# Gate and up of the last 1024 tokens by seven block products, with down as a stage of its own

## The chip, the cores and the metric

The kernel runs on one core of one Trainium2 chip. The metric is the device time of one launch in microseconds (us). Before the change three runs took 2739.67, 2743.64 and 2744.93 us; the median is 2743.64 us.

## The reference

One decoder layer on 2048 tokens of width 1024, all in float32. A token mixer (latent attention, a gated MLP in chunks, a short convolution) is followed by an output projection, and then a channel mixer:

```
h = rms_norm(x, ffn_pre_g)                                    # 2048 x 1024
f = (silu(h @ w_gate) * (h @ w_up)) @ w_down                  # 1024 -> 2816 -> 1024
x = x + rms_norm(f, ffn_post_g)
```

The change touches only this channel mixer, and only for tokens 1024 to 2047.

## The kernel before

Float32 accuracy is kept by splitting each operand into a high part and a rest (`hi_lo`, L164: ScalarE (ACT) rounds the high part, then VectorE (DVE) or GpSimd (POOL) subtracts it), and by three TensorE (PE) matmuls for each product: high x high, high x low, low x high (`mm3`, L203 to L205). A matmul here has 128 x 128 weights and 512 moving columns.

The stages follow each other: input projections, attention woven with the other mixers, the output projection and the first channel mixer (tokens 0 to 1023, `f0`), and then, from 1895 us on, the part that the change replaces or touches:

- `out_proj` for token tiles 8 to 15 (128 tokens each). For each tile it ends in `mix_post` (the normalised rows `h2`, L1038), eight transposes (L1045), two copies to `hT` (L1046) and a store to a DRAM tile `h2T_d` (L1048).
- `ffn(tail, 1, ...)`, called `f1`, for the 1024 tokens of tiles 8 to 15. `load_h2T` (L1129) reads `h2T_d` back and splits it into `h2T[0]` (tiles 8 to 11) and `h2T[1]` (tiles 12 to 15). Then eleven groups of two 128-wide column blocks j: `half` computes gate and up for one block and 512 tokens, 2 x 24 matmuls into PSUM tiles `gu`, then silu, product and split into `gT`. `down` multiplies the two blocks with `w_down` into PSUM tiles `pd` and adds each to an SBUF sum `acc` on DVE (L1173). Weights are read (L1116, L1139) and split once.
- `last_down` (L1203) has the last half and the last four token tiles: as each 512-wide piece of the output is complete, it is summed, squared, normalised and stored (L1233 to L1247).

All PE work of one half is 48 matmuls, so gate and up of these 1024 tokens are 22 blocks x 2 halves x 48 = 2112 matmuls, and down is 22 x 8 tiles x 2 x 3 = 1056.

Outside the places where an order is pinned, a list scheduler of the framework orders the instructions of each engine from its own estimate of times; each engine and each queue then runs its instructions strictly in that order and waits on semaphores. DMAs issued by SyncE (SP) are one such queue. Pools of SBUF tiles are opened on two sides; a tile that takes the place of an earlier one waits until that one has been used for the last time.

Of the kernel before, what the change touches and what calls it, by code (L numbers as in the profile page):

```python
# [11 lines left out]
F32 = mybir.dt.float32  # L12
F32R = mybir.dt.float32r
BF16 = mybir.dt.bfloat16
I32 = mybir.dt.int32
AF = mybir.ActivationFunctionType
ALU = mybir.AluOpType
AX = mybir.AxisListType

P = 128  # L20
S = 2048
D = 1024
KD = D // P
# [41 lines left out]
WB = 2  # L65
PAUSE3 = 8.0
WB1 = 1
H = 8
QR = 384
KVR = 256  # L70
FF = 2816
NF = FF // P
# [12 lines left out]
def trunk(  # L85
# [6 lines left out]
    nc = tc.nc  # L92
# [3 lines left out]
    x, out = x[0], out[0]  # L96
    w_in, w_uq, w_ukv, w_out = w_in[0], w_uq[0], w_ukv[0], w_out[0]
    w_gate, w_up, w_down = w_gate[0], w_up[0], w_down[0]

    const = ctx.enter_context(tc.tile_pool(name="const", bufs=1))  # L100
    dram = ctx.enter_context(tc.tile_pool(name="scratch", bufs=1, space=DRAM))
# [5 lines left out]
    def bank(tags, name):  # L107
        i = turn.get(tags, 0)
        turn[tags] = i + 1
        tag = tags[i % len(tags)]  # L110
        return psp.tile([P, 512], F32, name=name, tag=tag, bufs=BANKS[tag])
# [37 lines left out]
    hT_d = [dram.tile([P, 2, KD, P], F32R, name=f"hT_d{t}") for t in range(NT)]  # L149
    q_d = [dram.tile([H, 64, 2 * GT], F32R, name=f"q_d{c}") for c in range(S // GT)]  # L150
    qr_d = [dram.tile([P, 2, 2 * GT], F32R, name=f"qr_d{c}") for c in range(S // GT)]
    k_d = [dram.tile([H, 2, 96, 2, GT], F32R, name=f"k_d{c}") for c in range(NCH)]
    v_d = [dram.tile([P, 8, H, P], F32R, name=f"v_d{c}") for c in range(NCH // 2)]
    ya_d = [dram.tile([P, 2, 512], F32, name=f"ya_d{t}") for t in range(NT // 2)]
    ybc_d = [dram.tile([P, 512], F32, name=f"ybc_d{t}") for t in range(NT)]
    x2_d = [dram.tile([P, D], F32, name=f"x2_d{t}") for t in range(NT)]
    h2T_d = [dram.tile([P, KD, P], F32, name=f"h2T_d{t}") for t in range(NT)]
    trig_x = [dram.tile([H, 16, 2 * GT], F32, name=f"trig_x{c}") for c in range(S // GT)]
    trig_d = dram.tile([P, 2 * GT], F32, name="trig_d")

    def rows(t):
        return slice(t * P, (t + 1) * P)

    def hi_lo(hi, lo, src, eng=None):  # L164
        nc.scalar.activation(hi, src, AF.Copy)  # L165
        return (eng or nc.vector).tensor_tensor(lo, src, hi.bitcast(F32), op=ALU.subtract)  # L166

    def put(dst, src):
        nc.sync.dma_start(dst.bitcast(F32), src.bitcast(F32))

    def inv_rms(pool, ssq, n, width=1, bufs=8, eps=EPS, out=None):
        r = pool.tile([P, 4], F32, name="invr", tag="invr", bufs=bufs) if out is None else out
        nc.gpsimd.tensor_scalar(r[:, :width], ssq, 1.0 / n, eps, op0=ALU.mult, op1=ALU.add)
        nc.gpsimd.tensor_tensor(r[:, :width], r[:, :width], mhalf[:, :width], op=ALU.pow)
        return r
# [446 lines left out]
    with ExitStack() as ph:  # L622
# [31 lines left out]
        rp = rp_ctx.enter_context(tc.tile_pool(name="rope", bufs=1, side="right", reuse_waits="tile"))  # L654
# [618 lines left out]
                finish(t0, acc, range(ntc))  # L1273


    at_ctx = ctx.enter_context(ExitStack())
    at_pools.append(at_ctx.enter_context(tc.tile_pool(name="c_s", bufs=2, reuse_waits="tile")))
    next(rest)
# [3 lines left out]
    wo = []  # L1282
# [11 lines left out]
    with wo_ctx, ExitStack() as ph:  # L1294
        wo.append(wout_tiles(ph, 1, "d_wb", "right"))
        dsp = ph.enter_context(tc.tile_pool(name="d_s0", bufs=2, side="right", reuse_waits="tile"))
        gains = out_gains(ph, "d_g0", "right")
        dhp = ph.enter_context(tc.tile_pool(name="d_h0", bufs=1, side="right", reuse_waits="tile"))
        op0 = out_proj(dsp, dhp, None, wo, gains, range(0, 8), "z", "nx")
        next(op0)  # L1300
        wout_load(wo[1], 1, "d_stgb", "left", WB1)
        weave(op0, att, RATE1, LO_OUT, -PAUSE1)

    with ExitStack() as ph:
        def pools():
            return (ph.enter_context(tc.tile_pool(name="e_s0", bufs=2, side="right", reuse_waits="tile")),
                    ph.enter_context(tc.tile_pool(name="e_p0", bufs=1, side="right", reuse_waits="tile")))
# [6 lines left out]
        late = ctx.enter_context(ExitStack())  # L1314
        owed, wo = 0.0, None
# [11 lines left out]
        for cost in f0:  # L1327
            owed += RATE2 * cost
            while owed >= 1.0 and wo is None:
                owed -= 1.0  # L1330
                if not step(att):
                    wo, gains, dmp, mix = second_half()
        if wo is None:
            for _ in att:
                pass
            wo, gains, dmp, mix = second_half()

    with ExitStack() as tail:
        def pools():
            return (tail.enter_context(tc.tile_pool(name="e_s1", bufs=2, reuse_waits="tile")),  # L1340
                    tail.enter_context(tc.tile_pool(name="e_p1", bufs=1, reuse_waits="tile")))

        f1 = ffn(tail, 1, "right", (8,), 8, pools, "zszsz", "nox", False, 3)
        spare = next(f1)
        with ExitStack() as ph:
            dsp = ph.enter_context(tc.tile_pool(name="d_s1", bufs=2, side="right", reuse_waits="tile"))
            dhp = ph.enter_context(tc.tile_pool(name="d_h1", bufs=1, side="right", reuse_waits="tile"))
            op1 = out_proj(dsp, dhp, (dmp, spare[:, 3], mix), wo, gains, range(8, 16), "zzzs", "nox")
            next(op1)
            next(op1)  # L1350
            next(f1)
            for _ in op1:
                pass
        late.close()
        for _ in f1:
            pass
# [31 lines left out]
```

## Time and profile before

| | us |
|---|---|
| median of 3 runs | 2743.64 |
| the profiled execution, whole | 2746.96 |
| its span, first to last instruction | 2745.2 |
| PE busy in the span | 2651.7 (97%) |
| DVE, ACT, POOL busy | 1563.3, 1015.5, 727.0 |

A row of the timeline gives start, duration, engine, line, operation and, in brackets, the idle time before it with what ended it. PE's durations overlap: a matmul of 512 columns is shown with 0.39 us, while the next one starts 0.227 us later, so a pitch is read from two starts and never from a duration. Queue rows (SPq) show the issue of a DMA, not its transfer. In the profile the tiles `h2T0` and `h2T1` are both called `h2T`, and `x2` is `x`.

### The profile page before, as it was taken

What the parts mean: (1) busy time and instruction counts of PE and PEld (TensorE: products, weight loads), DVE (VectorE), ACT (ScalarE), POOL (GpSimd) and SP (SyncE); (2) the same over time, 40 slices, a digit from 0 to 9 for tenths busy, and PEclk for the clock granted to TensorE, in tenths of its full rate; (3) what the DMA queues carried; (4) which work ended last, traced back from release to release, by engine and by line L of the source; (5) the groups of instructions that cost most, each with busy time, mean ns of one, the idle gap of its engine ahead of it and who ended that gap; (6) DMA issues with size and microseconds to landing.
All of it is one profiled execution on the core that took longest, in us unless ns stands there. A gap on an engine that the chain in (4) does not pass through costs nothing. (4 is left out here: it accounts for less than half of the span.)

```text
span 2745.2 us, 37350 instructions
## 1 busy us (share of the span) xinstructions
PE 2651.7 (97%) x14076; PEld 2277.6 (83%) x14076; DVE 1563.3 (57%) x2709; ACT 1015.5 (37%) x1857; POOL 727.0 (26%) x828
## 2 busy tenths in 40 slices
PE   8999989999898999999999999999999999999998
PEld 7999868888777888888878888877878888888886
DVE  6555575566767666657677676764543333333335
ACT  6444344444546334444444444442531111111112
POOL 1222325666443232332343223313200000000004
PEclk9999979999999999999999999999999999999999
DMA  8756755444435332333253322254551111111113
GB/s 297 225 183 179 226 185 154 146 144 134 144 130 187 101 110 89 93 93 104 87 163 99 114 79 77 75 162 143 176 169 46 46 47 46 46 47 46 47 39 123
DMA packets 268945, 329.42 MB, mean 120 GB/s; under 512 B 17646, under 2 KB 198300, under 8 KB 264092
## 3 DMA queue, kind: packets, MB, share of 16 engines
q1 hardware_dynamic: 261244, 293.46, 34.5%
q0 software_dynamic: 5184, 29.36, 3.3%
q10 hardware_dynamic: 2336, 4.20, 0.4%
q8 instruction: 111, 1.82, 0.3%
q14 instruction: 70, 0.57, 0.1%
HBM read 238.56 MB, written 86.25 MB: 118 GB/s over the span
## 5 line engine op out<-in xcount | busy, mean ns | idle before, releaser
L476 POOL TENSOR_TENSOR pl<-p,ph 128x512 fp32r<-128x512 f32 (+1 forms) x240 | 325.8, 1362 | 636.8 <-ACT ph L473 542.2
L1173 DVE TENSOR_TENSOR acc<-pd,acc 128x512 f32<-128x512 f32 x304 | 206.1, 688 | 228.4 <-PE pd L205 227.9
L203 PE MATMUL gu<-h2T,wgh 128*128 128x512 f32 x704 | 275.1, 391 | 2.1 <-ACT h2T L165 2.1
L203 PE MATMUL gu<-h2T,wuh 128*128 128x512 f32 x704 | 275.2, 391 | 0.0
L204 PE MATMUL gu<-h2T,wgh 128*128 128x512 f32 x704 | 274.9, 391 | 0.1
L205 PE MATMUL gu<-h2T,wul 128*128 128x512 f32 x704 | 274.7, 390 | 0.0
L204 PE MATMUL gu<-h2T,wuh 128*128 128x512 f32 x704 | 274.7, 390 | 0.0
L205 PE MATMUL gu<-h2T,wgl 128*128 128x512 f32 x704 | 274.5, 390 | 0.0
L203 PE MATMUL pd<-wd,gT 128*128 128x512 f32 x672 | 265.0, 395 | 4.8 <-DVE acc L1173 2.7
L204 PE MATMUL pd<-wd,gT 128*128 128x512 f32 x672 | 262.3, 391 | 0.0
L205 PE MATMUL pd<-wd,gT 128*128 128x512 f32 x672 | 257.6, 392 | 0.3 <-DVE gT L166 0.3
L471 ACT ACTIVATE p<-sT 128x512 f32<-128x512 f32 (+1 forms) x288 | 163.3, 572 | 210.8 <-PE sT L205 120.7
L473 ACT ACTIVATE ph<-p 128x512 fp32r<-128x512 f32 (+1 forms) x288 | 174.2, 609 | 68.6 <-PE o L507 63.7
L1189 POOL DMA_DIRECT2D x<-x_d x8 | 4.7, 587 | 684.4 <-PE gu L205 683.1
L203 PE MATMUL sT<-zone 97*128 97x256 f32 x576 | 166.0, 288 | 7.5 <-ACT p L471 7.5
L435 DVE TENSOR_REDUCE mx<-s 128x1 f32<-128x512 f32 x192 | 130.2, 684 | 63.9 <-PE s L432 63.5
L205 PE MATMUL sT<-zone 97*128 97x256 f32 x576 | 165.1, 287 | 0.0
L204 PE MATMUL sT<-zone 97*128 97x256 f32 x576 | 165.0, 286 | 0.0
L507 PE MATMUL o<-pl,zone 128*128 128x256 f32 x576 | 151.5, 289 | 5.6 <-POOL pl L476 3.1
L165 ACT ACTIVATE gT<-sg 128x512 fp32r<-128x512 f32 x88 | 55.2, 627 | 274.4 <-DVE sg L1159 253.1
L203 PEld LDWEIGHTS gu<-h2T,wgh 128*128 128x128 f32 x704 | 132.3, 188 | 29.1 <-ACT h2T L165 2.5
L205 PEld LDWEIGHTS gu<-h2T,wul 128*128 128x128 f32 x704 | 132.5, 188 | 27.8
(280 smaller groups left out, 6293.2 us busy)
## 6 DMA issues: line engine op xcount, KB each, us to landing
raw<-in_w_gate_dram SPq DMA_DIRECT2D x66, 512.0 KB
raw<-in_w_up_dram SPq DMA_DIRECT2D x66, 512.0 KB
raw_d<-in_w_down_dram SPq DMA_DIRECT2D x66, 512.0 KB
ht<-hT_d POOLq DMA_DIRECT2D x20, 1024.0 KB, 5.7
zone<-k_d SPq DMA_DIRECT2D x48, 384.0 KB
hT_d<-ht SPq DMA_DIRECT2D x16, 1024.0 KB
xt<-in_x_dram SPq DMA_DIRECT2D x31, 512.0 KB
zone<-v_d SPq DMA_DIRECT2D x24, 512.0 KB
```

Source lines behind the costliest of these rows:

```text
L165: nc.scalar.activation(hi, src, AF.Copy)
L203: nc.tensor.matmul(ps, ah(k), bh(k), start=k == 0, stop=False)
L204: nc.tensor.matmul(ps, ah(k), bl(k), start=False, stop=False)
L205: nc.tensor.matmul(ps, al(k), bh(k), start=False, stop=k == n - 1)
L435: nc.vector.tensor_reduce(mx[:, b:b + 1], s[:, :w], axis=AX.X, op=ALU.max, negate=True)
L471: nc.scalar.activation(p[:, :w], s[:, :w], AF.Exp)
L473: nc.scalar.activation(ph_[:, :w], p[:, :w], AF.Copy)
L476: eng.tensor_tensor(pl_[:, :w], p[:, :w], ph_[:, :w].bitcast(F32), op=ALU.subtract)
L507: nc.tensor.matmul(o[:, at:256], vts[part, hd, j // 8][:, j % 8, :], pp[i][:, u * 256:u * 256 + 256 - at], start=j == 0 and i == 0, stop=j ...
L1173: nc.vector.tensor_tensor(acc[tt][:, cols], pd, acc[tt][:, cols], op=ALU.add)
L1189: nc.gpsimd.dma_start(x2, x2_d[t0 + tt])
```

## The change

`f1` is now `wide_ffn`. The weight matrices are cut in k (two halves of 512 rows) and in columns (blocks of 128, taken in pairs f = 0, 1), and the tokens in two halves of 512. For each pair i of column blocks, gate and up each form a 2 x 2 by 2 x 2 product of blocks, and this is done by the seven products of the Strassen-Winograd scheme in place of eight:

- `stage1(i)`: two products for each of gate and up with `b11` and `b21` (tiles 8 to 11, split into `b1`); they give the first output block.
- `stage2(i)`: five products for each, with `t2`, `t1`, `t3`, `t4` and `b22`. These five operands are sums and differences of the token blocks, made once from all eight `h2T_d` tiles in a loop over four pairs of tiles (`rx2`, two buffers), and each is split. On the weight side `s1`, `s2`, `s3` and a last difference are formed on POOL for each i, and every weight block is split as `aop` (five buffers).
- A product is 12 matmuls of 512 columns into one of all eight PSUM banks (`pw`). DVE adds the products up in SBUF (`plus`), ACT copies two of them.
- Each gated block is split and stored to DRAM (`gT_d`), 512 KB for a block and 512 tokens.

`stage1(0)` and `stage1(1)` come first, then the loop that makes the token operands, then `stage2(0)`, `stage2(1)`, and from i = 2 on both stages in turn.

Down is a stage after that, once for each half of the tokens: 8 PSUM banks hold the whole output of 512 tokens, and for each j of 22, `w_down` rows (512 KB) are loaded and split, `gT_d` (512 KB) is read back, and 24 matmuls add to the 8 banks. The last six j of the second half are held and done bank by bank. `w_down` is thus loaded and split twice. The SBUF sums `acc`, `down` and `last_down` are gone for these tokens; `f0` still uses `ffn`.

```diff
+LASTJ = 6
+    gT_d = [dram.tile([P, 2, 2, 512], F32R, name=f"gT_d{j}") for j in range(NF)]
+    ALL = "zsznzsox"
+    def wide_ffn(early, late, side, t0):
+        eap = early.enter_context(tc.tile_pool(name="w_a", bufs=5, side=side, reuse_waits="tile"))
+        b1 = ehp.tile([P, 2, KD, 512], F32R, name="b1")
+        yield b1[:, :, :, 384:512]
...
+        def operand(src):
+            a = eap.tile([P, 2, 4, P], F32R, name="aop")
+            hi_lo(a[:, 0], a[:, 1], src)
+            return a
+        def product(a, b):
+            ps = bank(ALL, "pw")
+            for k in range(4):
+                for i, (u, v) in enumerate(((0, 0), (0, 1), (1, 0))):
+                    nc.tensor.matmul(ps, a[:, u, k, :], b[:, v, k, :], start=k == 0 and i == 0,
+                                     stop=k == 3 and i == 2)
+            return ps
+        fetch(0)
...
+        fetch(1)
...
+        def gated(i, f, th, g, up):
+            nc.scalar.activation(g, g, AF.Silu)
+            nc.vector.tensor_tensor(g, up, g, op=ALU.mult)
+            gt = gp_.tile([P, 2, 512], F32R, name="gt")
+            hi_lo(gt[:, 0], gt[:, 1], g)
+            put(gT_d[2 * i + f][:, th], gt)
...
+            for m in range(2):
+                ps = product(operand(block(raws[i][m], 0, 0)), b11)
+                nc.scalar.activation(us[i][m], ps, AF.Copy)
...
+            for m in range(2):
+                plus(c11[m], product(operand(block(raws[i][m], 0, 1)), b21), us[i][m])
+            gated(i, 0, 0, *c11)
...
+        for i in range(2):
+            stage1(i)
+        with tc.tile_pool(name="w_x", bufs=2, reuse_waits="tile") as rp:
+            for tt in range(4):
+                r = rp.tile([P, 2, KD, P], F32, name="rx2")
+                for e in range(2):
+                    nc.sync.dma_start(r[:, e], h2T_d[t0 + 4 * e + tt])
...
+                nc.vector.tensor_tensor(x11, x12, x11, op=ALU.subtract)
+                nc.gpsimd.tensor_tensor(x12, x22, x12, op=ALU.subtract)
+                split(t1, x11)
+                nc.vector.tensor_tensor(x11, x22, x11, op=ALU.subtract)
+                split(t2, x11)
+                nc.vector.tensor_tensor(x21, x21, x11, op=ALU.subtract)
+                split(t3, x12, nc.gpsimd)
+                split(t4, x21)
+                split(b22, x22, nc.gpsimd)
...
+            for m in range(2):
+                s1.append(ssp.tile([P, 4, P], F32, name="sa"))
+                nc.gpsimd.tensor_tensor(s1[m], block(raw[m], 1, 0), block(raw[m], 1, 1), op=ALU.add)
+                s2.append(ssp.tile([P, 4, P], F32, name="sb"))
+                nc.gpsimd.tensor_tensor(s2[m], s1[m], block(raw[m], 0, 0), op=ALU.subtract)
+                plus(u[m], product(operand(s2[m]), t2), u[m])
+            for m in range(2):
+                p5.append(product(operand(s1[m]), t1))
+                plus(w[m], p5[m], u[m])
...
+        for i in range(n):
+            if i > 1:
+                stage1(i)
+            stage2(i)
+            if i + 2 < n:
+                fetch(i + 2)
...
+        def load(h, j):
+            pool = first if h == 0 and j < 2 else rest_
+            raw = pool.tile([P, D], F32, name="rawd", bufs=2 if pool is first else 3)
+            nc.sync.dma_start(raw, w_down[rows(j), :])
+            wd = pool.tile([P, 2, D], F32R, name="wd")
+            hi_lo(wd[:, 0], wd[:, 1], raw)
+            gt = pool.tile([P, 2, 512], F32R, name="gtl")
+            put(gt, gT_d[j][:, h])
+            return gt, wd
...
+                junk = op.tile([P, 512], F32, name="junk", bufs=2)
+                nc.scalar.activation(junk, ps, AF.Square, accum_out=sq[:, nn:nn + 1])
+                nc.vector.tensor_tensor(ag[:, cols], ps, g_po[:, cols], op=ALU.mult)
...
+            pds = {(tt, nn): bank(ALL, "pd") for tt in range(4) for nn in range(2)}
+            held = []
+            for j in range(NF):
+                gw = load(h, j)
+                if h == 1 and j >= NF - LASTJ:
+                    held.append(gw)
+                    continue
+                for (tt, nn), ps in pds.items():
+                    add(ps, gw, tt, halves[nn], j)
+                    if j == NF - 1:
+                        ended(tt, nn, ps)
+            for (tt, nn), ps in pds.items() if held else ():
+                for i, gw in enumerate(held):
+                    add(ps, gw, tt, halves[nn], NF - LASTJ + i)
+                ended(tt, nn, ps)
...
-        f1 = ffn(tail, 1, "right", (8,), 8, pools, "zszsz", "nox", False, 3)
+        f1 = wide_ffn(first, tail, "right", 8)
```

How the order changes, at two places. Up to the first matmul of the output projection of tiles 8 to 15, PE's instructions are the same in both programs; from there to the end it has 13,618 - 10,209 = 3,409 in place of 3,673, that is 264 fewer.

The first place is SP's queue at the end of the output projection. `h2T_d8` to `h2T_d15` are the stored tiles 8 to 15. Before:

```order
L1081 DMA xt_20490<-in_x_dram 128x1024
L1133 DMA raw_h_20595<-h2T_d13_182 128x1024
L1048 DMA h2T_d14_183<-hT_20534 128x1024
L1036 DMA x2_d15_168<-xt_20490 128x1024
L1133 DMA raw_h_20599<-h2T_d14_183 128x1024
L1048 DMA h2T_d15_184<-hT_20548 128x1024
L1133 DMA raw_h_20603<-h2T_d15_184 128x1024
L1139 DMA raw_d_20837<-in_w_down_dram 128x1024
L1139 DMA raw_d_20843<-in_w_down_dram 128x1024
L1116 DMA raw_20849<-in_w_gate_dram 128x8x128
L1116 DMA raw_20855<-in_w_up_dram 128x8x128
L1116 DMA raw_20861<-in_w_gate_dram 128x8x128
```

And now (`rx2` are the reads for the token operands, `raww` the weights of `fetch(1)`, `xt` the residual rows):

```order
L1050 DMA h2T_d14_183<-hT_20536 128x1024
L1038 DMA x2_d15_168<-xt_20492 128x1024
L1360 DMA rx2_20766<-h2T_d8_177 128x1024
L1360 DMA rx2_20766<-h2T_d12_181 128x1024
L1360 DMA rx2_20783<-h2T_d9_178 128x1024
L1360 DMA rx2_20783<-h2T_d13_182 128x1024
L1050 DMA h2T_d15_184<-hT_20550 128x1024
L1295 DMA raww_20587<-in_w_gate_dram 128x8x256
L1295 DMA raww_20589<-in_w_up_dram 128x8x256
L1360 DMA rx2_20800<-h2T_d10_179 128x1024
L1360 DMA rx2_20800<-h2T_d14_183 128x1024
L1360 DMA rx2_20817<-h2T_d11_180 128x1024
L1360 DMA rx2_20817<-h2T_d15_184 128x1024
```

Before, each stored tile was read back right after its store, and the weights of the first two blocks had been loaded earlier. Now four reads stand ahead of the store of tile 15, the weights for `stage1(1)` (2 MB) stand behind it, and the last four reads stand behind those; the fifth read waits until both splits of the first `rx2` buffer that come last (`t4` on DVE, `t3` on POOL) are done.

The second place is DVE behind the last normalised rows `h2` of the output projection. Before (`raw_h` are the tiles read back, `sg` and `gT` the gated block):

```order
L1038 SCALAR_TENSOR_TENSOR h2_20433<-xt_20490,invr_20530,g_fp_18967 128x1024
L1159 TENSOR_TENSOR sg_20667<-gu_20642,sg_20667 128x512
L166 TENSOR_TENSOR gT_20615<-sg_20667,gT_20615 128x512
L166 TENSOR_TENSOR h2T1_20574<-raw_h_20591,h2T1_20574 128x1024
L166 TENSOR_TENSOR h2T1_20574<-raw_h_20595,h2T1_20574 128x1024
L166 TENSOR_TENSOR h2T1_20574<-raw_h_20599,h2T1_20574 128x1024
L1159 TENSOR_TENSOR sg_20722<-gu_20697,sg_20722 128x512
L166 TENSOR_TENSOR h2T1_20574<-raw_h_20603,h2T1_20574 128x1024
L166 TENSOR_TENSOR gT_20616<-sg_20722,gT_20616 128x512
L166 TENSOR_TENSOR wd1_20840<-raw_d_20837,wd0_20839 128x1024
L166 TENSOR_TENSOR wd1_20846<-raw_d_20843,wd0_20845 128x1024
```

And now, from the third row of the token operands on (`aop_20687` is the first weight operand of `stage1(1)`, `c0` and `c1` are the results of `stage1(0)`, `pw` a product):

```order
L1367 TENSOR_TENSOR rx2_20783<-rx2_20783 128x512
L1372 TENSOR_TENSOR rx2_20766<-rx2_20766 128x512
L168 TENSOR_TENSOR t2_20574<-rx2_20766,t2_20574 128x4x128
L168 TENSOR_TENSOR t1_20573<-rx2_20783,t1_20573 128x4x128
L168 TENSOR_TENSOR t4_20576<-rx2_20766,t4_20576 128x4x128
L1370 TENSOR_TENSOR rx2_20783<-rx2_20783 128x512
L1340 TENSOR_TENSOR c0_20643<-pw_20648,u0_20607 128x512
L1340 TENSOR_TENSOR c1_20644<-pw_20665,u1_20608 128x512
L1372 TENSOR_TENSOR rx2_20783<-rx2_20783 128x512
L168 TENSOR_TENSOR t2_20574<-rx2_20783,t2_20574 128x4x128
L1334 TENSOR_TENSOR c0_20643<-c1_20644,c0_20643 128x512
L168 TENSOR_TENSOR aop_20687<-raww_20587,aop_20687 128x512
```

Four splits and the gated block stood there; now the low part of the first weight operand of `stage1(1)` stands behind fourteen other operations that need the reads of both `rx2` buffers and the last products of `stage1(0)`. Behind it the same pattern follows for the other two `rx2` pairs, with the first operand of `stage2(0)` at its end. From the fifth product of `stage2(0)` on, the operand of a product stands at least five products ahead of its use in DVE's and ACT's order.

## Rows read from the trace of the kernel before

**Rows 1.** The page: busy time, share and instructions of each engine.

```profile
PE 2651.7 (97%) x14076; PEld 2277.6 (83%) x14076; DVE 1563.3 (57%) x2709; ACT 1015.5 (37%) x1857; POOL 727.0 (26%) x828
```

**Rows 2.** Windows: stretch, us, busy of each engine (count), granted clock, DMA share, GB/s.

```profile
2016.00:2031.30 15.30, 13.25 (x63) 10.73 (x61) 5.59 (x7) 6.26 (x9) 0.00 (x0) 1.00 0.31 104
2031.30:2733.00 701.70, 700.60 (x3072) 576.29 (x3072) 260.64 (x330) 122.81 (x173) 23.72 (x32) 1.00 0.18 56
2733.00:2745.20 12.20, 0.02 (x1) 0.00 (x0) 7.84 (x11) 2.06 (x6) 6.47 (x9) 0.64 0.46 172
```

**Rows 3.** Timeline of PE, 2720 us to the end.

```profile
2725.02 8.00 PE L1219 MATMUL pd<-wd,gT 128*128 128x512 f32 x34 [1.03 <-DVE gT L166]
```

**Rows 4.** Timeline of PE, 2015 to 2120 us.

```profile
2020.27 1.03 PE L1045 MATMUL tr<-ident,h 128*128 128x128 f32 x8
2031.30 0.50 PE L203 MATMUL gu<-h2T,wgh 128*128 128x512 f32 x1 [2.05 <-ACT h2T L165]
```

**Rows 5.** Timeline of PE, 1860 to 2130 us.

```profile
1862.12 0.39 PE L203 MATMUL gu<-h2T,wgh 128*128 128x512 f32 x1
1883.89 11.09 PE L1219 MATMUL pd<-wd,gT 128*128 128x512 f32 x48
1898.30 0.51 PE L203 MATMUL pp<-wo,h2T 128*128 128x512 f32 x1 [2.44 <-ACT h2T L165]
```

**Rows 6.** Timeline of DVE, 2720 us to the end.

```profile
2740.14 2.06 DVE L1245 SCALAR_TENSOR_TENSOR ag<-ag,invr,x 128x512 f32<-128x512 f32 x3
```

**Rows 7.** Queue of SP, 2720 us to the end: issue of DMAs.

```profile
2732.16 10.40 SPq L1247 DMA_DIRECT2D out_dram<-ag  x8
```

**Rows 8.** ACT's groups by shape, whole span: count, busy us, mean ns, idle before.

```profile
L165 ACT ACTIVATE gT<-sg 128x512 fp32r<-128x512 f32 x88 | 55.2, 627 | 274.4 <-DVE sg L1159 253.1 <-DVE sg L1156 21.1
```

**Rows 9.** Timeline of POOL, 2720 us to the end.

```profile
2738.41 0.65 POOL L1242 TENSOR_TENSOR sql<-sql 128x1 f32<-128x1 f32 x1
2739.74 0.88 POOL L174 TENSOR_TENSOR invr<-invr,mhalf 128x1 f32<-128x1 f32 x1
```

**Rows 10.** DVE's groups by shape, 2032 to 2700 us.

```profile
L1173 DVE TENSOR_TENSOR acc<-pd,acc 128x512 f32<-128x512 f32 x144 | 99.4, 691 | 182.9 <-PE pd L205 182.9
L166 DVE TENSOR_TENSOR gT<-sg,gT 128x512 fp32r<-128x512 f32 x41 | 28.2, 687 | 14.0 <-ACT gT L165 14.0
L166 DVE TENSOR_TENSOR wd<-raw_d,wd 128x1024 fp32r<-128x1024 f32 x22 | 26.9, 1221 | 34.8 <-ACT wd L165 34.7
```

**Rows 11.** POOL's groups by shape, whole span.

```profile
L476 POOL TENSOR_TENSOR pl<-p,ph 128x512 fp32r<-128x512 f32 x192 | 273.6, 1429 | 567.3 <-ACT ph L473 475.5 <-PE sT L205 30.0 <-DVE gT L166 14.6
```

**Rows 12.** Windows of 5 and 20 us: columns as in rows 2.

```profile
20.00:40.00 20.00, 18.97 (x127) 18.30 (x126) 18.64 (x45) 15.73 (x39) 6.37 (x14) 1.00 0.99 383
1900.00:1905.00 5.00, 4.88 (x14) 3.93 (x15) 4.93 (x7) 0.00 (x0) 3.18 (x4) 0.66 0.25 93
2030.00:2035.00 5.00, 3.63 (x15) 2.67 (x16) 3.16 (x4) 3.71 (x4) 0.00 (x0) 1.00 0.72 248
```

**Rows 13.** Timeline of ACT, 2000 to 2085 us.

```profile
2006.64 0.60 ACT L1086 ACTIVATE h<-pp 128x512 f32<-128x512 f32 x1 [4.02 <-PE pp L205]
2009.47 1.28 ACT L1158 ACT_TABLE_LOAD   x1
2030.19 1.06 ACT L165 ACTIVATE h2T<-raw_h 128x1024 fp32r<-128x1024 f32 x1 [2.91 <-DMA raw_h<-h2T_d]
```

**Rows 14.** Queue of SP, 2000 to 2085 us.

```profile
2026.68 0.32 SPq L1133 DMA_DIRECT2D raw_h<-h2T_d  x1
```

**Rows 15.** DMA issues, 2690 to 2745 us: size of each, median us to landing.

```profile
x<-x_d POOLq DMA_DIRECT2D x8, 512.0 KB, 4.9
```

**Rows 16.** Timeline of DVE, 2000 to 2085 us.

```profile
2014.66 1.28 DVE L1038 SCALAR_TENSOR_TENSOR h<-xt,invr,g_fp 128x1024 f32<-128x1024 f32 x1 [2.68 <-POOL invr L174]
```

**Rows 17.** DVE's groups by shape, 1700 to 1895 us, while POOL works beside it.

```profile
L166 DVE TENSOR_TENSOR wo<-raw,wo 128x512 fp32r<-128x512 f32 x16 | 15.2, 961 | 7.0 <-ACT wo L165 7.0
L495 DVE TENSOR_TENSOR acc<-acc,p 128x512 f32<-128x512 f32 x12 | 14.5, 1211 | 2.1 <-ACT p L471 2.0
```

More of the change, by code (lines that the diff above doesn't have):

```diff
@@ L1336, in trunk @@
             wo, gains, dmp, mix = second_half()
[L1338 to L1341, printed above, removed]
-        f1 = ffn(tail, 1, "right", (8,), 8, pools, "zszsz", "nox", False, 3)
+    with ExitStack() as tail, ExitStack() as first:
+        f1 = wide_ffn(first, tail, "right", 8)
         spare = next(f1)
@@ L1347, in trunk @@
             dhp = ph.enter_context(tc.tile_pool(name="d_h1", bufs=1, side="right", reuse_waits="tile"))
-            op1 = out_proj(dsp, dhp, (dmp, spare[:, 3], mix), wo, gains, range(8, 16), "zzzs", "nox")
+            op1 = out_proj(dsp, dhp, (dmp, spare, mix), wo, gains, range(8, 16), "zzzs", "nox")
             next(op1)
```

84 lines of the change are left out of this document (added).

## The prediction

> **What bounds the kernel now.** I read the page first: PE is busy for 2651.7 of 2745.2 us, 97%, and no other engine, its own weight loads aside, for more than 57% [rows 1]. Time is saved here only by fewer matmuls or fewer holes between them. Then the windows of the part that changes. From 2031.30 us to the last matmul at 2733.0 us PE runs 3072 matmuls with 700.6 busy us [rows 2] and one wait of 1.0 us [rows 3]; in front of it stands one hole of 2.05 us [rows 4], and behind the last matmul 12.2 us in which PE has nothing to do [rows 2]. DVE works 260.6 us of these 701.7, ACT 122.8, POOL 23.7, and the DMA engines 18% [rows 2]: there is room beside PE. The unit of the sum comes from the PE timeline: from the gate-up matmul at 1862.12 to the `pd` matmul at 1883.89 there are 96 starts, so 0.2268 us each [rows 5]. For the 2016 gate-up matmuls in the window that makes 457.2 us, and the 1056 of down have the rest, 0.2305 each.
>
> **What goes.** (1) Seven products for eight takes 264 of the 2112 gate-up matmuls, all with 512 columns: 264 x 0.2268 = 59.9 us off PE. PE is on the path throughout, so it counts in full if nothing else comes late. (2) The wait of 1.0 us ahead of the last matmuls [rows 3] has no place in the new order: -1. (3) The tail. Now 34 matmuls of the last pieces run in 8.0 us [rows 3], which is faster than DVE and POOL finish them: DVE ends at 2742.2 [rows 6] and the last store is issued at about 2742.5 [rows 7], 9.5 us behind PE. In the new order the last pieces come 18 matmuls, 4.1 us, apart, so nothing is queued up. The last chain is then one square on ACT, about as long as a split (0.63, [rows 8]) and its read-out, three small POOL operations (2.2 from 2738.41 to 2740.62, [rows 9]), two DVE steps (1.4, two thirds of the 2.06 of [rows 6]) and a store (2.7, from its issue to the end): some 7 us for 12.2. That is -5, bounds -3 and -7.
>
> **What is hidden.** In the steady part a pair takes 168 matmuls = 38.1 us on PE. DVE has 14 PSUM sums at 0.691, and 22 splits and products of SBUF data at 0.687 [rows 10]: 24.8 us. ACT has 24 steps of about 0.63 [rows 8], 15 us, POOL 8 at 1.43 [rows 11], 11.4 us. The operands stand five products, 13.6 us, ahead. All that lies beside PE: 0. The DMAs of a pair are 2 MB of weights and 2 MB of stores, 110 GB/s; the trace shows 383 GB/s over 20 us [rows 12].
>
> Down reads 1 MB for each j, which is 24 x 0.2305 = 5.5 us of PE: 190 GB/s, half of those 383. One 512 KB load lands 3.5 us after its issue alone [rows 13, 14] and 4.9 in a crowd [rows 15], its split takes 1.06 on ACT and 1.22 on DVE [rows 10, 13], and eight buffers stand ahead: 0. At its start, the load for j = 2 stands on SP behind the store of the last gated block, about 3 us after the last product; with 4.9 and 2.3 that is 10.2 us, and j = 0 and 1 cover 11. At the seam of the two halves the eight banks are read by ACT and DVE while PE comes back to them after 5 us; DVE has eight products, some late splits and the first sums to do: I take +1 for both, bounds 0 and 5. The pitch of a product (a new bank every 12 matmuls) lies between 0.2268 and 0.2306 [rows 3, 5]; 0 here, bounds -4 and +4.
>
> **What is added: a hole at the head.** Before, 96 gate-up matmuls stood between the end of the output projection and the first that needs tiles 12 to 15, and their weights were there. The same number stands there now, but only 48 of them have their weights. The output projection's last result is read at 2006.64 [rows 13]. By the new order PE then has 32 matmuls and 8 transposes, 8.3 us, to 2014.8, waits for the last `h2` at 2015.9 [rows 16] (1.1 us), does the 8 transposes of tile 15 (1.03, [rows 4]) and the last 12 matmuls of `stage1(0)`, and is out of work at 2019.7.
>
> `stage1(1)` can start when ACT has split its first weights. In ACT's order this stands behind a `t2` split that needs the ninth DVE operation behind the first reads. The reads are issued from 2016 on; 3.5 us for the first and 1.4 for each more (0.5 MB at 383 GB/s) puts the second pair at 2021 and the fourth read at 2024. Nine DVE operations take 6.2 us at 0.687; beside a working POOL the trace has 0.961 for a split [rows 17], which makes 8.6. Then ACT has a split, a table load of 1.28 [rows 13], a silu and the operand, 3.1 us: 2030.3 to 2032.8. The 2 MB of weights stand behind 2.6 MB and land at about 2030 too. I take 12 us of idle time. 48 matmuls later, with 1 us more for the first low part, it is 2043.6.
>
> The first operand of `stage2(0)` stands behind fifteen more DVE operations from the other four reads, which go out only when the first two buffers are free: 10.3 to 14.4 us from about 2035.5, then two ACT steps, 2047 to 2051. POOL comes to the same: 15 operations of 1.43 from 2021.6 are 21.4 us, and some 5 us of waiting for the reads lie between. I take 6 us. Together 1 + 12 + 1 + 6 = 20 us for the 2.05 of before: +18. Bounds: +6 if the reads come earlier than I put them and POOL does not slow DVE; +28 if all DVE operations take the 1.211 us of the worst group [rows 17] (15 and 13 us of idle time).
>
> On this the Trainium skill has a rule that speaks against the change. The page SBUF — State Buffer (section Who interferes with whom) says that a DVE instruction with two SBUF inputs and a GpSimd instruction that reads SBUF exclude each other for their whole length. The trace agrees in kind (0.961 and 1.211 beside POOL, 0.687 without). Taken to the letter, POOL's six operations would be added to DVE's nine in the first idle stretch, some 15 us in place of 8.6, and the sum would be 6 us higher.
>
> (4) The clock. After the wait of 2.44 us that ended at 1898.30 [rows 5] the granted clock from 1900 to 1905 is 0.66, so a part of these 5 us ran at 1.2 GHz, the lower level: 14 matmuls took 4.9 busy us for 3.2 [rows 12]. After the 2.05 us at 2031 it stayed at 1.00 [rows 12]. For two long holes I take +3, bounds 0 and 7.
>
> **Sum.** -59.9 - 1 - 5 + 1 + 18 + 3 = -43.9 us against the profiled execution of 2746.96 us, which stands 3.3 us over the median. Against the median: 2743.6 - 43.9 = 2700.
>
> **Rivals.**
> - The hole is small: the scheduler has laid reads and splits so that PE waits under 8 us. For it speaks that the transfers have room; against it that in DVE's order the operands of `stage1(1)` and of `stage2(0)` stand behind results of the product before them. Hole +6, no loss of clock: 2685.
> - The hole is larger, each link slowed by the others. The long DVE chain between two products speaks for it, the short splits of 0.687 against it: +28, and 6 for the clock: 2713.
> - DVE becomes the bound of the product loop, because it can't work while POOL reads SBUF. In `stage2` alone DVE has 16 x 0.687 + 12 x 0.691 = 19.3 us, with POOL's 11.4 added 30.7, for 27.2 of PE: 3.5 us over. In the whole pair it is 36.2 for 38.1, so the five operands in hand should carry it. If they don't, 11 x 3.5 = 38 us come back: 2738. By the rule that the Trainium skill gives on its page SBUF — State Buffer this is the worst case, and no row here shows it.
> - Slower than before: the feed of down becomes the bound. It needs 46.1 MB in 44 x 5.5 = 242 us. Below 162 GB/s (284 us) the gain is gone; at 150 GB/s it is 307 us and 2765 in all. For it speaks that a single 512 KB load at a time would give only 107 to 150 GB/s (4.9 and 3.5 us each); against it that loads overlap at 383 GB/s and that up to eight blocks may be ahead.
> - That the change doesn't do what it says is excluded by the order: PE has 264 instructions fewer, and the rest have the same shape.
>
> **Chances.** Forecast (2690 to 2712) 0.62; small hole 0.15; larger hole 0.11; DVE bound 0.08; feed bound 0.04. A measurement can tell about 0.2%, 5.5 us, from no change, so faster means under 2738: the first three and most of the fourth, 0.93; same 0.02; slower 0.05. The range reaches from the small hole to a larger one with some of the DVE bound: 2684 to 2723.
>
> **What the profile after would show.** PE: 1848 `pw` matmuls 0.227 apart. One or two idle stretches of together some 20 us between 2015 and 2055, the first ended by ACT or DVE on `aop`, the second likewise; a granted clock under 1 behind them. No waits of PE on DVE from there to down, none of more than 2 us at its start and its seam. About 7 us from the last matmul to the end. If the first hole is ended by the DMA of `raww`, my chain over DVE is wrong though the size may hold. If PE waits in every pair, the DVE bound was right; if PE waits for `wd` or `gtl` in many j, the feed was.

## The result and the profile after

The changed kernel takes 2707.62 us (median of 4 runs, 2706.94 to 2712.53) against 2741.88 (4 runs beside it): a ratio of 0.9878, 95% interval [0.9861, 0.9895], 34 us faster. The forecast was 2700, with a range of 2684 to 2723. The direction and the range held; the gain is some 10 us smaller than forecast.

The profiled executions are 40.0 us apart, and that is not all the change. This is the page of the changed kernel, then windows of each kernel (columns as in [rows 2]), first before, then after. They are cut where the matmul behind a short wait (0.3 us) in the last `down` of the first channel mixer begins; up to there both run the same 10222 matmuls.

```profile
PE 2592.3 (96%) x13812; PEld 2227.2 (82%) x13812; DVE 1653.1 (61%) x2855; ACT 1110.3 (41%) x2027; POOL 853.0 (32%) x921
```

```profile
0.00:1855.10 1855.10, 1782.86 (x10222) 1563.09 (x10222) 1211.73 (x2275) 817.32 (x1544) 656.77 (x718) 0.98 0.46 140
```

```profile
0.00:1847.10 1847.10, 1778.92 (x10222) 1559.77 (x10222) 1209.07 (x2275) 817.58 (x1544) 656.02 (x718) 0.98 0.46 141
1847.10:2010.00 162.90, 153.19 (x714) 125.65 (x714) 75.63 (x89) 63.32 (x124) 39.09 (x70) 0.97 0.43 150
2010.00:2054.40 44.40, 17.44 (x68) 13.45 (x68) 33.77 (x36) 21.25 (x36) 25.91 (x16) 0.74 0.53 178
2054.40:2468.50 414.10, 414.03 (x1800) 339.20 (x1800) 262.00 (x382) 153.11 (x250) 120.35 (x90) 0.99 0.32 113
2698.70:2705.20 6.50, 0.01 (x1) 0.00 (x0) 2.11 (x3) 0.69 (x2) 0.93 (x3) 0.65 0.21 81
```

The untouched part ended 8.0 us earlier in one execution than in the other. That is scatter, so every comparison below begins at this cut, the **mark**: from it to the end the kernel before takes 2745.2 - 1855.1 = 890.1 us and the changed one 858.1. The change is worth 32.0 us there, which fits the medians. Read the last three columns of work from top to bottom: PE has 264 instructions fewer (14076 [rows 1] to 13812), is busy 17.44 of 44.40 us at the head, without a hole in the product loop, and the tail is 6.5 us for 12.2 [rows 2].

All waits of PE behind the mark, on the timeline of the changed kernel (start, us, operation, count, idle before it and what ended it). They answer to [rows 3 to 5]:

```profile
1892.13 0.80 PE L205 MATMUL pp<-wo,b 128*128 128x512 f32 x1 [4.35 <-ACT b L167]
1897.46 0.79 PE L207 MATMUL pp<-wo,b 128*128 128x512 f32 x1 [3.25 <-DVE b L168]
1912.51 0.50 PE L205 MATMUL pp<-wo,mT 128*128 128x512 f32 x1 [1.29 <-ACT mT L167]
2010.06 1.06 PE L1047 MATMUL tr<-ident,h 128*128 128x128 f32 x8 [0.86 <-DVE h L1040]
2011.42 3.03 PE L1310 MATMUL pw<-b,aop 128*128 128x512 f32 x12 [0.30 <-ACT hT L1048]
2030.40 13.35 PE L1310 MATMUL pw<-b,aop 128*128 128x512 f32 x48 [15.95 <-ACT aop L167]
2054.47 24.47 PE L1310 MATMUL pw<-t,aop 128*128 128x512 f32 x96 [10.73 <-ACT aop L167]
2469.97 30.41 PE L1437 MATMUL pd<-wd,gtl 128*128 128x512 f32 x133 [1.47 <-DMA gtl<-gT_d]
```

The kernel before has these waits at the start of the output projection, beside the 2.44 of [rows 5]:

```profile
1900.12 0.80 PE L205 MATMUL pp<-wo,h2T 128*128 128x512 f32 x1 [0.61 <-DVE h2T L166]
1913.20 0.66 PE L196 MATMUL tr<-ident,mix 128*128 128x128 f32 x4 [0.72 <-DVE mix L1019]
1914.67 0.66 PE L196 MATMUL tr<-ident,mix 128*128 128x128 f32 x4 [0.81 <-DVE mix L1019]
1916.56 0.51 PE L203 MATMUL pp<-wo,mT 128*128 128x512 f32 x1 [1.24 <-ACT mT L165]
```

From these rows the 32 us come apart. Every measured entry is a difference after minus before.

| term | forecast | measured | from |
|---|---|---|---|
| 264 matmuls fewer | -59.9 | -59.9 | counts; 0.2268 each [rows 5] |
| wait ahead of the last matmuls | -1 | -1.0 | no such wait is left |
| tail | -5 | -5.7 | 6.5 for 12.2 |
| start and seam of down | +1 | +1.5 | 1.47 on `gtl`, none at the seam |
| waits at the head | +18 | +25.8 | 0.86 + 0.30 + 15.95 + 10.73 = 27.84 for 2.05 [rows 4] |
| slow matmuls behind these waits | +3 | +5.2 | 48 in 13.35 for 10.9, 96 in 24.47 for 21.8; each row ends with the shown 0.39 us of its last matmul, so 0.3 us of this is overlap |
| start of the output projection | 0 | +3.1 | 4.35 + 3.25 + 1.29 = 8.89 for 2.44 + 0.61 + 0.72 + 0.81 + 1.24 = 5.82 |
| rest | 0 | -0.9 | what is left to the sum |
| sum | -43.9 | -31.9 | |

The small rest hides two opposite entries. From 2457.44 to 2698.72 us down's 1056 matmuls take 239.8 busy us, 0.2271 each, for the 0.2305 that the prediction worked out for the kernel before: -3.6. In the steady loop the products are 0.2278 apart (439 in 100 us) for 0.2268: some +2. The prediction had put the pitch at 0 with bounds of -4 and +4.

So three places have to be explained: the head, the matmuls behind it, and a seam that the prediction never looked at.

What stands in the head? These are DVE's operations on the tokens, then POOL's and ACT's in the same stretch, of the changed kernel:

```profile
2015.15 0.69 DVE L1367 TENSOR_TENSOR rx<-rx 128x512 f32<-128x512 f32 x1 [5.24 <-DMA rx<-h2T_d]
2020.45 5.10 DVE L168 TENSOR_TENSOR t<-rx,t 128x512 fp32r<-128x512 f32 x3
2025.47 1.75 DVE L1370 TENSOR_TENSOR rx<-rx 128x512 f32<-128x512 f32 x1
2048.47 0.68 DVE L168 TENSOR_TENSOR t<-rx,t 128x512 fp32r<-128x512 f32 x1
```

```profile
2021.63 1.71 POOL L1368 TENSOR_TENSOR rx<-rx 128x512 f32<-128x512 f32 x1
2049.28 3.26 POOL L1385 TENSOR_TENSOR sa<-raww 128x512 f32<-128x512 f32 x2 [4.28 <-issue]
2052.50 2.48 POOL L1387 TENSOR_TENSOR sb<-sa,raww 128x512 f32<-128x512 f32 x2
```

```profile
2027.25 0.63 ACT L167 ACTIVATE t<-rx 128x512 fp32r<-128x512 f32 x1 [3.26 <-DVE rx L1370]
2053.79 0.63 ACT L167 ACTIVATE aop<-sb 128x512 fp32r<-128x512 f32 x1 [3.38 <-POOL sb L1387]
```

DVE's first operation, begun ahead of POOL's, takes 0.69 us. While POOL works back to back, an operation of DVE on two SBUF tiles takes 1.63 to 1.78, in step with POOL's 1.71. Alone both are shorter: DVE's 0.687 [rows 10], POOL's 1.28 (`sa` at 2054.88 us in the kernel with the early sums below, where DVE stands still beside it). The 1.429 of [rows 11] is a mean over the whole span, with DVE at work in a part of it.

The first wait ends as predicted, by ACT, behind a split that needs DVE's ninth operation. The second ends by another chain than predicted: POOL's `sa` begins 0.1 us after DVE's last token split (2048.47 + 0.68), and two `sa`, one `sb` and a split on ACT follow it.

### The profile page after: what moved, and what is told of

It reads as the page before. It is cut to its first block, busy times and chain, and to the rows that moved or that the text cites. A ratio compares the mean times of both kernels' runs of the same rounds, so it can differ in the third digit from the quotient of the medians.

```text
span 2705.2 us, 37665 instructions
## 1 busy us (share of the span) xinstructions
PE 2592.3 (96%) x13812; PEld 2227.2 (82%) x13812; DVE 1653.1 (61%) x2855; ACT 1110.3 (41%) x2027; POOL 853.0 (32%) x921
## 5 line engine op out<-in xcount | busy, mean ns | idle before, releaser
L1310 PE MATMUL pw<-t,aop 128*128 128x512 f32 x1056 | 246.0, 394 | 10.7 <-ACT aop L167 10.7
L1310 PEld LDWEIGHTS pw<-t,aop 128*128 128x128 f32 x1056 | 199.5, 189 | 55.5 <-ACT aop L167 11.2
L1437 PE MATMUL pd<-wd,gtl 128*128 128x512 f32 x1056 | 239.8, 389 | 1.5 <-DMA gtl<-gT_d 1.5
L1437 PEld LDWEIGHTS pd<-wd,gtl 128*128 128x128 f32 x1056 | 198.1, 188 | 43.0 <-ACT wd L167 1.9
L1310 PE MATMUL pw<-b,aop 128*128 128x512 f32 x792 | 185.7, 394 | 16.2 <-ACT aop L167 15.9
L1310 PEld LDWEIGHTS pw<-b,aop 128*128 128x128 f32 x792 | 150.0, 190 | 49.3 <-ACT aop L167 16.4
L509 PE MATMUL o<-ph,zone 128*128 128x256 f32 x576 | 151.8, 284 | 2.5 <-ACT os L515 2.5
L205 PE MATMUL gu<-h2T,wuh 128*128 128x512 f32 x352 | 137.9, 392 | 0.0
L205 PE MATMUL gu<-h2T,wgh 128*128 128x512 f32 x352 | 137.8, 391 | 0.0
L207 PE MATMUL gu<-h2T,wul 128*128 128x512 f32 x352 | 137.6, 391 | 0.0
L206 PE MATMUL gu<-h2T,wuh 128*128 128x512 f32 x352 | 137.5, 391 | 0.0
L206 PE MATMUL gu<-h2T,wgh 128*128 128x512 f32 x352 | 137.5, 391 | 0.0
```

The lines of the kernel that those rows point to most:

```text
L205: nc.tensor.matmul(ps, ah(k), bh(k), start=k == 0, stop=False)
L206: nc.tensor.matmul(ps, ah(k), bl(k), start=False, stop=False)
L207: nc.tensor.matmul(ps, al(k), bh(k), start=False, stop=k == n - 1)
L509: nc.tensor.matmul(o[:, at:256], vts[part, hd, j // 8][:, j % 8, :], pp[i][:, u * 256:u * 256 + 256 - at], start=j == 0 and i == 0, stop=j ...
L1310: nc.tensor.matmul(ps, a[:, u, k, :], b[:, v, k, :], start=k == 0 and i == 0, stop=k == 3 and i == 2)
L1437: nc.tensor.matmul(ps, gt[:, a, rows(tt)], wd[:, b, cols], start=j == 0 and i == 0, stop=j == NF - 1 and i == 2)
```

## The experiments

Theory A: POOL and DVE hold each other up, and that lengthens DVE's chain. B, its rival: the transfers set the end. C: POOL's sums wait for memory. D: the seam's wait comes from the place of a split in ACT's and DVE's order. E: the granted clock falls while PE waits, and the next matmuls pay. "From the mark" means from the same matmul as above to the end: 858.1 us in the changed kernel. Each such figure is of one execution. Up to tile 15's transposes the changed kernel and five of those below do the same work; they took 162.3 to 163.0 us from the mark, so a difference of about 1 us is not clear of scatter.

### POOL kept out of the token loop

```
+nc.gpsimd.memset(t[:, 1].bitcast(F32), 0.0)              # for t3 and b22, ahead of the loop
...
-nc.gpsimd.tensor_tensor(x12, x22, x12, op=ALU.subtract)
...
-split(t3, x12, nc.gpsimd)
-split(b22, x22, nc.gpsimd)
+nc.scalar.activation(t3[:, 0, :, cols], x12, AF.Copy)    # and b22 from x22
```

> Left out: POOL's subtraction x12 and its two low parts (t3, b22) of each tile; the low halves are zeroed by POOL ahead of the loop, so t3 and b22 hold other numbers. DVE and ACT keep all their operations. The changed kernel waits 27.8 us in all from the last transposes to the first product of stage2 (15.95 and 10.73 and two short ones), and DVE's operations on two SBUF inputs take 1.63 to 1.78 us there beside POOL, 0.69 alone. Theory A (POOL and DVE lock each other out, and DVE's chain sets the end): the operations fall to 0.69, some 5 us go out of each wait, 16 to 19 us are left. Theory B (the reads of the tiles and of the weights set the end, DVE's length is a symptom): the waits shrink by under 2 us.

DVE's groups in this kernel, 2019 to 2050 us, and PE's two waits:

```profile
L168 DVE TENSOR_TENSOR t<-rx,t 128x512 fp32r<-128x512 f32 x12 | 8.1, 688 | 2.2 <-ACT t L167 2.2
L1369 DVE TENSOR_TENSOR rx<-rx 128x512 f32<-128x512 f32 x4 | 2.8, 692 | 8.1 <-DMA rx<-h2T_d 8.1
```

```profile
2032.78 14.20 PE L1310 MATMUL pw<-b,aop 128*128 128x512 f32 x48 [11.63 <-ACT aop L167]
2053.69 25.37 PE L1310 MATMUL pw<-t,aop 128*128 128x512 f32 x96 [6.71 <-ACT aop L167]
```

The same operations take 0.69 us each, and 19.5 us of waiting are left of 27.8 (with 0.86 and 0.30), just above A's 16 to 19. From the mark it is 851.6 us; the median is 2703.17 us (0.9853 [0.9831, 0.9875]), of a kernel that leaves out work. A holds for 8 us of waiting, B falls as the main cause; but DVE now waits 8.1 us for the reads, so the transfers come close behind.

### The same work, all on DVE

```
-nc.gpsimd.tensor_tensor(x12, x22, x12, op=ALU.subtract)
+nc.vector.tensor_tensor(x12, x22, x12, op=ALU.subtract)
...
-split(t3, x12, nc.gpsimd)
+split(t3, x12)                                           # and b22
```

> Same work, but POOL's three operations of each tile are given to DVE. Theory A (lock): a DVE and a POOL operation side by side took 1.70 us for the pair, two on DVE take 2 x 0.69 = 1.38, so twelve pairs save 12 x 0.32 = 4 us: waits of 22 to 26 us for 27.8. Theory B (POOL is a second pair of hands, and the transfers bound): twelve more operations of 0.69 on DVE are 8.3 us more, waits of 30 to 36 us.

```profile
2030.61 1.22 PE L1310 MATMUL pw<-b,aop 128*128 128x512 f32 x2 [11.40 <-ACT aop L167]
2032.17 12.07 PE L1310 MATMUL pw<-b,aop 128*128 128x512 f32 x46 [0.34 <-DVE aop L168]
2054.42 24.49 PE L1310 MATMUL pw<-t,aop 128*128 128x512 f32 x96 [10.17 <-ACT aop L167]
```

That is PE's timeline: 23.1 us of waiting. Twelve operations more on DVE made the head shorter, 853.2 us from the mark, 2704.10 us in all, ratio 0.9859 [0.9840, 0.9877] (its interval overlaps that of the changed kernel; the trace decides). This is A's number; B wanted 30 to 36.

### The first sums made early

```
+ab = ehp.tile([P, KD, P], F32, name="rh")       # sa, sb and their split, ahead of the loop
+nc.gpsimd.tensor_tensor(sa0, block(raws[0][0], 1, 0), block(raws[0][0], 1, 1), op=ALU.add)
+nc.gpsimd.tensor_tensor(sb0, sa0, block(raws[0][0], 0, 0), op=ALU.subtract)
+op0 = operand(sb0)
...                                               # used for the first product of stage2(0)
```

> The sums sa and sb of the first operand of stage2(0) go into a tile outside the memory of the token reads and are made, with their splits, ahead of the token loop. Theory C (the end of the second wait is set by the memory that sa takes over from the token reads: POOL's sa starts at 2049.28, 0.2 us after the last read of it, and sa, sa, sb and a split follow, 5.2 us): the second wait ends some 5 us earlier, 5 to 6.5 us for 10.73. Rival (the last token split on DVE, or the transfers, set it): under 1.5 us change.

```profile
2050.58 0.79 PE L1310 MATMUL pw<-t,aop 128*128 128x512 f32 x1 [4.39 <-ACT t L167]
2051.84 4.36 PE L1310 MATMUL pw<-t,aop 128*128 128x512 f32 x11 [0.47 <-DVE t L168]
2058.09 21.47 PE L1310 MATMUL pw<-t,aop 128*128 128x512 f32 x84 [1.89 <-ACT aop L167]
```

C holds for the wait: the second one is 4.39 us for 10.73 and ends with a token split. But the next operands are late too (0.47 and 1.89), and the first 12 matmuls run slowly, so that from the mark it is 857.2 us, 0.9 less, which is within the scatter (2710.15 us, 0.9881 [0.9861, 0.9901]). A wait that is shortened at its front alone is not yet time.

### The pool of b1 aligned

```
+rhp = early.enter_context(tc.tile_pool(name="w_p", bufs=2, ...))   # ahead of the pool of b1
-rh = ehp.tile([P, KD, P], F32, name="rh")
+rh = rhp.tile([P, KD, P], F32, name="rh")
-gp_, cp = left("w_g", 2), left("w_c", 2)
+gp_, cp = left("w_g", 1), left("w_c", 2)
```

> The tile rh goes into a pool of its own with two buffers, so that the pool of b1 lies wholly in memory that the last gate-up left; gt gets one buffer for two to make room. This puts the split of tile 8's transposes on ACT and DVE where the kernel before has it. The changed kernel waits 4.35 and 3.25 us for this split at the start of the output projection, the one before 2.44 and 0.61. Theory D (the place of the split in ACT's and DVE's order makes the wait): 3 to 3.5 us for 7.6, the stretch to tile 15's transposes 3 to 5 us shorter, total 3 to 5 us less. Rival (DVE and POOL are just as late with the last rows of down): no change; and if one buffer for gt is too few, PE waits in every pair and the total rises.

The seam on ACT, first in the changed kernel, then in this one: the split `b<-tr` stands behind the last square of `acc`, or between them.

```profile
1890.87 0.63 ACT L1237 ACTIVATE junk<-acc 128x512 f32<-128x512 f32 x1 [1.20 <-DVE acc L1235]
1891.50 1.07 ACT L167 ACTIVATE b<-tr 128x512 fp32r<-128x512 f32 x2
```

```profile
1899.16 0.60 ACT L167 ACTIVATE b<-tr 128x512 fp32r<-128x512 f32 x1 [1.10 <-PE tr L198]
1900.73 0.63 ACT L1237 ACTIVATE junk<-acc 128x512 f32<-128x512 f32 x1 [0.97 <-DVE acc L1235]
```

```profile
1901.99 0.79 PE L205 MATMUL pp<-wo,b 128*128 128x512 f32 x1 [2.43 <-ACT b L167]
```

D holds: PE waits 2.43 us for 7.60 at this place. Two waits on `mix` come in behind it (1.37 and 1.49), and to tile 15's transposes it is 159.3 us from the mark for 163.0. The total does not show it (2711.45 us, 0.9871 [0.9842, 0.9900]); from the mark it is 856.6, 1.5 less, since from those transposes to the end it took 2.2 us more (697.4 for 695.1). Whether the single buffer of `gt` has a part in that was not told apart; no wait of PE shows it.

### The three together

The edits of the last three runs, with `sa` and `sb` of both first operands in the two buffers of `rh`.

> Three things at once: all token operations on DVE (POOL silent in the loop), sa and sb of both first operands of stage2(0) in tiles outside the token reads' memory and made ahead, and the pool of b1 aligned as in the aligned run. Theory A, C and D together: waits at the start of the output projection 2.4 to 3 us for 7.6; first long wait about 11.5, second 4 to 6 (10.17 with DVE alone), so some 17.5 us in all from the last transposes to stage2 for 27.8. From the wait in the last down block of the first half to the end 842 to 848 us for 858.1, and 2693 to 2698 us in all. Rival: what the second wait loses comes back as waits of the next products and as a lower clock, as where only the early sums were made (4 us of wait went, 1 us of time): 852 us, 2700 or more.

```profile
2025.81 1.22 PE L1311 MATMUL pw<-b,aop 128*128 128x512 f32 x2 [11.77 <-ACT aop L167]
2027.22 11.78 PE L1311 MATMUL pw<-b,aop 128*128 128x512 f32 x46 [0.19 <-DVE aop L168]
2040.85 0.51 PE L1311 MATMUL pw<-t,aop 128*128 128x512 f32 x1 [1.85 <-ACT aop L167]
2043.87 25.28 PE L1311 MATMUL pw<-t,aop 128*128 128x512 f32 x95 [2.52 <-DVE t L168]
```

With 0.87 and 0.30 these are 17.5 us of waiting, the number expected; 842.8 us from the mark, 15 less than the changed kernel. 2696.30 us, ratio 0.9817 [0.9801, 0.9832]: faster than both kernels, since the interval lies below that of the changed one too. Together they give more (15.3) than one by one (4.9 + 0.9 + 1.5). The trace says where: to tile 15's transposes it is 157.9 us for 163.0, 5.0 less, and from there to the end 10.3 less. In the head each edit alone had left the other's chain in charge: with all on DVE the second wait was still ended by POOL's sums (10.17), with early sums by DVE's token splits.

### Extra matmuls while PE would wait

```
+def idle_work(n):                                # behind stage1(0) and stage1(1)
+    ps = bank(ALL, "pw")
+    with tc.issue_after(last[0].ins):
+        for k in range(n):
+            nc.tensor.matmul(ps, b1[:, 0, k % 8, 0:P], b1[:, 0, k % 8, :], ...)
```

The number of extra matmuls is given for each place in the expectations. First with the three edits, then with nothing else changed.

> The kernel with the three edits, and 44 and 16 extra matmuls on b1 into a bank that nothing reads, queued behind stage1(0) and stage1(1), where PE would only wait. Theory E (the granted clock falls while PE waits, and that costs some 2.5 us behind each of the two waits: 48 matmuls took 13.35 us and 96 took 24.47, at 0.227 they are 10.9 and 21.8): the clock stays at 1.00, 48 in about 11 and 96 in about 22, 4 to 5 us less than without the extra matmuls. Rival (the first matmuls behind a wait are slow since their operands come late, not for the clock): no gain, or a loss where the extra matmuls outlast the wait.

> The changed kernel with nothing but 62 and 40 extra matmuls on b1 into an unread bank, in place of its two long waits (15.95 and 10.73 us; 14.1 and 9.1 us at 0.227 each). It prices the term of the clock alone. Theory E: the granted clock stays at 1.00 through both waits, the 48 products behind the first take about 11 us for 13.35, the 96 behind the second about 22 for 24.47; from the wait in the last down block of the first half to the end 852 to 854 us for 858.1, 4 to 6 us less in all. Rival (those matmuls were slow for late operands): 13 and 24 us as before, no change in time.

A window of 5 us within the first wait (columns as in [rows 2]), of the kernel with the three edits and of the same with the extra matmuls; then PE's timeline behind the last wait of the second, and behind both waits in the kernel with the extra matmuls alone:

```profile
2020.00:2025.00 5.00, 0.00 (x0) 0.00 (x0) 4.86 (x9) 4.32 (x7) 0.00 (x0) 0.50 1.03 335
```

```profile
2020.00:2025.00 5.00, 3.17 (x13) 2.03 (x12) 5.00 (x10) 4.61 (x8) 0.00 (x0) 1.00 0.95 299
```

```profile
2041.54 22.02 PE L1311 MATMUL pw<-t,aop 128*128 128x512 f32 x95 [2.44 <-DVE t L168]
```

```profile
2034.78 12.68 PE L1310 MATMUL pw<-b,aop 128*128 128x512 f32 x48 [2.27 <-ACT aop L167]
2058.66 0.73 PE L1310 MATMUL pw<-t,aop 128*128 128x512 f32 x2 [2.14 <-ACT aop L167]
2059.78 21.80 PE L1310 MATMUL pw<-t,aop 128*128 128x512 f32 x94 [0.39 <-DVE aop L168]
```

In the first wait the granted clock stays at 1.00 instead of falling to 0.50, the lower level (1.2 GHz). Behind the last wait the 95 matmuls take 22.02 us for 25.28. But the gain is smaller than E said: 839.0 us from the mark for 842.8 with the three edits, 856.7 for 858.1 alone; the medians (2693.76, 0.9810 [0.9793, 0.9826], and 2709.16, 0.9866 [0.9844, 0.9888]) cannot tell.

Where did the rest go? These are windows behind the first wait, of the changed kernel and of the same with the extra matmuls alone:

```profile
2030.00:2035.00 5.00, 4.60 (x11) 3.52 (x12) 4.76 (x8) 3.67 (x8) 1.46 (x1) 0.50 0.40 96
```

```profile
2035.00:2040.00 5.00, 5.00 (x16) 3.85 (x17) 4.30 (x8) 3.67 (x8) 2.08 (x1) 0.70 0.57 144
```

In the second the extra matmuls had ended 2.27 us ahead of the first operand, and the clock fell behind this gap all the same: 0.70 over these 5 us, in which 16 matmuls ran where 22 fit at 0.227. So the 48 matmuls still took 12.68 us for 13.35, and this run does not price the first wait's clock. The kernel with the three edits and the extra matmuls does: with the clock at 1.00 throughout, 46 matmuls took 10.74 us, close to full pitch, for 11.78. The excess of these was the clock; late operands, the rival, have only the short waits ahead of them (1.03 and 0.80 us). Yet it is not time: stage2 begins 44.6 us behind the transposes for 44.4 (extra matmuls alone), and 34.2 for 34.2 (with the three edits), because the tokens set it. Only what is slow behind the last wait is time. There the clock stayed at 1.00 in both, and the 96 matmuls of the kernel with the extra matmuls alone took 22.9 us, with a pause of 0.39 for an operand, for 24.47.

### Down alone

Gate and up by eight block products, each over all eight k-tiles, with the same gated store and the same down stage:

```
-t1, t2, t3, t4, b22                              # and stage1, stage2
+b2 = tp.tile([P, 2, KD, 512], F32R, name="b2")   # tiles 12 to 15, split like b1
+def eight(i, th, b):                             # 8 products of 12 matmuls for each th
```

> The down stage of the change alone: gate and up of the last 1024 tokens by eight block products (2112 matmuls as before), through the same gated store and the same down stage. Theory (the hole at the head is the price of the seven products, down by itself gives the tail and costs little): waits of under 4 us from the last transposes to the first product on tiles 12 to 15, tail near 6 us for 12.2, the rest as before: 2735 to 2740 us against 2742 before. Rival (the down stage has a gain or a loss of its own that the sum missed, as its round trip of the gated blocks): 2725 or 2750.

PE has no wait between 1916 us and down, which starts with the only one left:

```profile
2500.79 219.47 PE L1389 MATMUL pd<-wd,gtl 128*128 128x512 f32 x967 [2.68 <-DMA gtl<-gT_d]
```

2739.95 us, ratio 0.9980 [0.9971, 0.9990]; 885.4 us from the mark, 4.7 less than before. So the down stage is worth 5 us, and the seven products 27.3 (885.4 - 858.1) of their 59.9: the hole at the head is wholly theirs. The seam is not: this kernel has it too (4.37, 3.25 and 1.25 us at the start of the output projection), so its 3.1 us are already taken off the 5.

### No blocks held back for the end

`LASTJ = 0` for 6.

> LASTJ = 0 for 6: all 44 blocks of down are added j by j, so the eight results are complete within the last 24 matmuls, 5.5 us. Theory: the eight read-outs queue up on ACT, DVE and POOL, and from the last matmul to the end it is 10 to 12 us for 5.8, total 4 to 6 us more than the changed kernel, 2712 to 2714. Rival (one read-out and its store set the tail whatever came before): 6 to 7 us, no change in time.

PE's last row, and DVE's in this kernel:

```profile
2697.64 4.70 PE L1437 MATMUL pd<-wd,gtl 128*128 128x512 f32 x20
```

```profile
2706.01 2.73 DVE L1458 SCALAR_TENSOR_TENSOR ag<-ag,invr,x 128x512 f32<-128x512 f32 x4
```

DVE ends 6.4 us behind PE, and the tail is 9.5 us (2702.3 to 2711.8) for 6.5. From the mark it is 862.4, 4.3 more, 3.0 of them in the tail. 2714.87 us, ratio 0.9886 [0.9871, 0.9901], which the interval of the changed kernel overlaps. The queue of read-outs is real in the trace, a little under the 10 to 12 expected.

## Where the prediction was right and where it failed

**Right.** The unit of the sum, the 264 matmuls, the tail, the vanished wait and the cover of the steady part: from 2054 to 2468 us PE is busy all 414 us, so the rival of a DVE bound by POOL did not come true; nor did that of a starved down, in which PE waits once, for 1.47 us. The two holes stand where they were put, each ended by ACT on `aop`, and the first one's chain is the predicted one, link by link.

**The hole: the chain was right, two of its prices were not.** The step "nine operations ... which makes 8.6" took from 2015.15 to 2027.2, 12.1 us: 0.961 was taken for an operation beside POOL, the row of a stretch in which POOL worked now and then; where POOL works back to back it is 1.7, and five of the nine took that. The upper row, 1.211, was still too low. By the rule on the Trainium skill's page SBUF — State Buffer (section Who interferes with whom), which the prediction weighed and did not take, this part came to some 15 us. The trace lies between: a pair in step takes 1.70, not 0.69 + 1.28 = 1.97. The step for the second hole, "POOL comes to the same", missed what POOL does next: its sums of weights lie in memory that the token reads give back, so they start only when DVE is done, and cost 5.2 us more up to the first product. 25.8 for 18 is nearest to the rival of a larger hole (+28). That the time still fell into the range is due to these wide bounds of the hole, not to the two prices.

**The clock: the mechanism was right, the size is partly luck.** Forecast +3, measured 5.2 us of slow matmuls. But about half of these stand behind the first wait, where they cost no time, because the tokens set the start of `stage2`. What came back with the clock held up behind the last wait is the price in time: 1.4 us in this kernel, little more than the scatter, and 3.8 in the one with the three edits.

**The seam: a step that was missing.** The prediction followed the moved instructions from the head on. The scheduler had also moved the first split of the output projection, more than 90 us ahead of the first product of the new code, and PE waited 3.1 us longer there.

Still open: what a further edit should take from the first wait, which stays at 11.4 to 11.8 us once POOL is out of the loop. In the kernel with the three edits its last 5.1 us are ACT's: two copies (the row below), three token splits, a table load, a silu, and the split that PE waits for (2025.14), one behind the other without a gap.

```profile
2020.65 1.09 ACT L1349 ACTIVATE u<-pw 128x512 f32<-128x512 f32 x2 [1.06 <-DMA h2T_d<-hT]
```

ACT began them behind a wait for the store of tile 15. The transfers that end with the 2 MB of weights ran at 346 GB/s until 2024.5 and at 146 in the next half microsecond, 1 us ahead of the wait's end; in the changed kernel they had fallen to 88 GB/s at 2025.0, 5 us ahead of it. So a shorter chain on ACT might soon wait for the weights instead; it was not tried.

## What to carry to other kernels

Price an operation that runs beside another engine's work on SBUF by a row in which both work without a pause, not by a mean of a mixed stretch. For each operand at a hole's end ask whose memory it takes over. Compare the order of every engine from the first row that differs, not from the first new line; and before a second pair of hands is used, add up what both hands take in step: here giving POOL's share to DVE was the faster way.

## What the runs showed of the hardware

DVE and POOL operations on two SBUF tiles each, 128x512, run in step at 1.70 us for the pair (0.69 and 1.28 alone), so POOL's help costs DVE 1.0 us an operation. ACT's operations took 0.63 us in the same stretch as elsewhere. Matmuls whose result nobody reads kept the granted clock at 1.00 through a wait of 11 us (0.50 without them); where they ended 2.27 us too early, it was 0.70 in the 5 us that followed, and 1.00 behind other gaps of 2.14 and 2.44 us.
